# A decoder layer on one core: elementwise work leaves GpSimd, index look-up by a minimum, part of the one-hots on ScalarE

## Chip, core and metric

One core of a Trainium2 chip runs the whole layer as one program. The metric is the device time of one execution in microseconds (us), lower is better. The engines are named as in the profile: PE is TensorE's matmul stream and PEld its weight loads, DVE is VectorE, ACT is ScalarE, POOL is GpSimd, SP is SyncE, which here only issues DMAs.

## What is computed

The reference is one post-norm decoder layer over 512 tokens of width 2048, in float32. Cut to what matters here:

```python
x1 = layer_norm(ALPHA * x + mix)                       # mix: pooling and gated linear attention, projected
q = (x1 @ w_query).reshape(T, 8, 2, 128)               # 8 heads, two halves
s, idx = top_k(einsum(q, sub_keys), 16)                # 16 of 128 keys per half
top_s, sel = top_k(s[:, :, 0, :, None] + s[:, :, 1, None, :], 16)
expert = idx0[sel // 16] * 128 + idx1[sel % 16]        # 128 picks a token, of 16384 experts
gate = softmax(top_s)
h = gelu(einsum('tkd,td->tk', u_tab[expert], x1))
y = einsum('tk,tkd->td', gate * h, v_tab[expert])
ple = sigmoid(x1 @ ple_w_gate) * (p @ ple_w_proj)
out = layer_norm(ALPHA * x1 + y + ple)
```

## The kernel before

Every large float32 matrix product is made of three passes over rounded halves (`mm3`): ACT casts a loaded 128x1024 piece to its high part (`shi` or `bigh`, L74), DVE or POOL subtracts that from the piece to get the low part (`slo` or `bigl`, L75), and PE runs high-high, low-high and high-low. A piece that comes late in either half stops PE at L93 or L95.

The stages follow one another in the program, and a scheduler orders the instructions of each engine in advance; on the chip each engine runs its own list in order. What matters here:

- **Norm stage** (near 618 to 668 us). `layer_norm` runs on DVE (L363 multiplies by the weight, L364 adds the bias, 128x2048 each), and for the token block `tt == 1` the add runs on POOL. The low parts for the small products with `ple_proj` and for the query chunks are POOL's.
- **Query stage** (near 668 to 868 us). Sixteen feature chunks of 48 matmuls; their low parts are POOL's (`nc.gpsimd` in the call of `feature_chunk`). Beside it runs `select`, a generator that is advanced between half chunks: per head DVE finds the top 16 (L441 to L445), turns positions into numbers, and looks the key indices up with a one-hot: DVE compares (`oh`, L484), POOL multiplies by the indices (L486), DVE sums (L487). It ends in `eidx` (L490).
- **Gate stage** (near 868 to 1215 us). Sixteen chunks with `ple_gate` (`ple_block`), each followed by a sigmoid on ACT and by products and residual adds on DVE (L627 to L631). Between half chunks a hook advances `routing`: for each group of four tokens DVE makes gate one-hots A1 (four of L652) and index one-hots A2 (one L654), PE multiplies them (L668), ACT copies the result into `stage` (L669), and a DMA writes it to memory. Groups are made two ahead. The hook also takes 1.5 sparse steps: POOL gathers the 128 rows of one pick (L527, an indirect DMA), and DVE takes their dot product with x1 (L544).
- **Dense stage** (near 1235 to 3042 us). 128 experts' columns at a time, all products for tokens 192 to 511, with `LOOK = 4` pieces split ahead. Each piece is a tick that also takes about 0.68 sparse steps for tokens 0 to 191: 128 dots and 128 adds for the first set (128 tokens), 64 of each for the second set (64 tokens, two copies side by side on the partitions). `x` for the second set goes into the buffer (`xs`) of the first.
- **Tail**. `first_out` and `second_out` normalize the two sparse sets. The second one adds its two copies with a product with a `fold` matrix on PE. They stand near the end of the list of items; after the list three blocks of dense tokens are transposed, normalized (`finish`) and written.

Of the kernel before, what the change touches and what calls it, by code (L numbers as in the profile page):

```python
# [10 lines left out]
F32 = mybir.dt.float32  # L11
# [9 lines left out]
P = 128  # L21
T = 512
# [29 lines left out]
def layer_kernel(ctx: ExitStack, tc: tile.TileContext, I, out):  # L52
# [301 lines left out]
    def layer_norm(dst, src, stats, w, b, pool, add_eng=None):  # L354
# [9 lines left out]
        (add_eng or nc.vector).tensor_add(dst, dst, b)  # L364

    with tc.tile_pool(name="outp", bufs=2, reuse_waits="tile") as op, tc.tile_pool(name="outc", bufs=1, reuse_waits="tile") as oc:
# [4 lines left out]
        for nb in range(4):  # L371
            sl = slice(nb * 512, (nb + 1) * 512)
            pss = token_block(I["w_out"][nb], YTh, YTl, pre=mixed if nb == 0 else None)
            if nb == 0:
# [10 lines left out]
                split(pTh, pTl, load_half(I["pT"]).rearrange("p (c t) -> p c t", c=2), nc.gpsimd)  # L385
# [6 lines left out]
        for q in range(4):  # L392
            wh, wl = load_split(I["ple_proj"][q], nc.gpsimd)
# [40 lines left out]
    iota = load_const("iota", [P, P], pool=sc1)  # L434
    i1a = sc1.tile([P, NT, NPICK], F32, name="i1a")
# [12 lines left out]
    def select(hd, s):  # L448
# [7 lines left out]
        nc.vector.tensor_copy(sif, si)  # L456
# [75 lines left out]
    def sparse_steps():  # L532
# [20 lines left out]
        nc.sync.dma_start(out=x[0], in_=x1d[0])  # L553
        for j in range(NPICK):
            step("u_rows", eidx, j, dot(x, hcol, j))
            yield
        x = [None]
        for j in range(NPX):
            step("u_rows", eidx1, j, dot(x, hcol1, j, PX), PX)
            if j == NROW - 1:  # L560
                x[0] = sp_.tile([P, D], F32, tag="xs", name="xs")
                for k in range(REP):
                    nc.sync.dma_start(out=x[0][k * NX:(k + 1) * NX, :], in_=x1d[1, :NX, :])
                nc.scalar.activation(hcol, hcol, AF.Gelu)
            if j == 9:
                nc.vector.tensor_mul(hcol, hcol, gate0)
            yield
        for j in range(NPICK):
            step("v_rows", eidx, j, add(accs[0], hcol, j))
            if j == NROW:  # L570
# [3 lines left out]
                nc.scalar.activation(hcol1[:PX], hcol1[:PX], AF.Gelu)  # L574
            if j == 9:
                nc.vector.tensor_mul(hcol1[:PX], hcol1[:PX], gate1[:PX])
# [44 lines left out]

    def ple_block(nb):
        for j in range(4):
# [5 lines left out]
            for dst, cs in ((baseS[:, f, P:], slice(P, NS)), (baseT[:, f, :], slice(NS, T))):  # L629
                for xx in (x1h, x1l):  # L630
                    mark[0] = nc.vector.scalar_tensor_tensor(dst, xx[:, f, cs].bitcast(F32), ALPHA, dst,  # L631
                                                             op0=ALU.mult, op1=ALU.add)


    def routing(tt):
# [8 lines left out]
        i1T, i2T, gT = tps  # L644
        B4 = [P, 4, P]
        lane = iota.unsqueeze(1).broadcast_to(B4)

        def onehots(t0):
            A1 = rt.tile(B4, F32, name="A1", bufs=3)
            A2 = rt.tile(B4, F32, name="A2", bufs=3)  # L650
            for t in range(t0, t0 + 4):
                nc.vector.tensor_scalar(A1[:, t - t0, :], iota, i1T[:, t:t + 1], gT[:, t:t + 1],  # L652
                                        op0=ALU.is_equal, op1=ALU.mult)
# [63 lines left out]
    with ExitStack() as es:  # L717
# [9 lines left out]
        def paced_split(src):  # L727
# [8 lines left out]
            mark[0] = split(hi, lo, raw)  # L736
# [207 lines left out]
```

## Time and profile before

| | |
|---|---|
| time, median of 3 runs | 3084.13 us (3079.32 to 3084.88) |
| the profiled execution: time, span | 3077.86 us, 3076.1 us |
| PE busy | 2941.5 us of the span |
| DVE busy | 2395.9 us |
| ACT busy | 1057.9 us |
| POOL busy | 748.4 us |

The span is from the first to the last instruction, and 1.8 us of the execution lie outside it. Busy times are summed over stages that have different limits, so the shares say little by themselves: a stage is read from which engine is full in it and from what the others wait for.

### The profile page before, as it was taken

To read this page: it belongs to the slowest core of one execution; us is meant where nothing else is said; L and a number is where in the kernel's file an instruction comes from. 1 tells how busy PE (TensorE), PEld (TensorE's weight loads), DVE (VectorE), ACT (ScalarE), POOL (GpSimd) and SP (SyncE) were. 2 spreads that over 40 slices of the span, in tenths; PEclk is the share of its full clock that TensorE was granted. 3 is DMA by queue.
4 is the path that set the end of the run, shared out by engine and by line. 5 is a ranking of instruction groups with operands and counts; after the bars stand their busy time and mean duration, and the time that the engine had idled before them with its cause. 6 is when DMAs were issued, how large, how long until landed. Compare 5 with 4: busy or idle time off the path is not lost.

```text
span 3076.1 us, 44401 instructions
## 1 busy us (share of the span) xinstructions
PE 2941.5 (96%) x17637; PEld 2743.0 (89%) x17637; DVE 2395.9 (78%) x3468; ACT 1057.9 (34%) x1290; POOL 748.4 (24%) x474
## 2 busy tenths in 40 slices
PE   9999999989987888999999999999999999999996
PEld 7878788878766776999999999999999999999996
DVE  3353733268889998998897898898988888989876
ACT  3232331152222443433333333333333333433332
POOL 0000400045522112222223222222223223222210
PEclk9999999999998889999999999999999999999998
DMA  5222133332247677999999999999999999999982
GB/s 200 103 103 103 58 135 123 111 110 76 83 147 265 260 254 271 392 371 370 365 361 345 372 364 371 356 373 362 367 364 367 368 360 362 374 360 369 356 302 89
DMA packets 206657, 833.74 MB, mean 271 GB/s; under 512 B 19105, under 2 KB 60577, under 8 KB 153522
## 3 DMA queue, kind: packets, MB, share of 16 engines
q1 hardware_dynamic: 107058, 386.29, 34.3%
q0 software_dynamic: 55296, 402.68, 33.9%
q10 hardware_dynamic: 44096, 41.95, 4.1%
q8 instruction: 138, 2.26, 0.3%
q14 instruction: 69, 0.57, 0.1%
HBM read 800.36 MB, written 30.41 MB: 270 GB/s over the span
## 4 chain that ended last, share of the span: by engine, by line
PE 69%; issue 14%; DVE 9%; POOL 5%; DMA 2%; ACT 1%; POOLq 0%; ACTq 0%; SPq 0%; DVEq 0%
PE ps L95 22%; PE ps L93 22%; PE ps L94 22%; POOL row L527 4%; DMA row<-in_u_rows,eidx 2%; DVE row L544 2%; DVE A L652 2%; DVE A L654 1%; DVE slo L75 1%; PE ps L612 0%; DVE basev L363 0%; DVE attnT L242 0%; DVE basev L364 0%; DVE E L265 0%; ACT shi L74 0%
## 5 line engine op out<-in xcount | busy, mean ns | idle before, releaser
L74 ACT CAST shi<-raw 128x1024 fp32r<-128x1024 f32 x474 | 498.8, 1053 | 1210.5 <-PE ps L94 880.2
L75 DVE TENSOR_TENSOR slo<-raw,shi 128x1024 fp32r<-128x1024 f32 x438 | 533.9, 1222 | 418.8 <-ACT shi L74 411.3
L95 PE MATMUL ps<-bigh,slo 128*128 128x320 f32 (+1 forms) x2016 | 697.7, 346 | 40.1 <-DVE slo L75 33.5
L93 PE MATMUL ps<-bigh,shi 128*128 128x320 f32 (+1 forms) x2016 | 697.6, 346 | 11.1 <-ACT shi L74 7.3
L94 PE MATMUL ps<-bigl,shi 128*128 128x320 f32 (+1 forms) x2016 | 696.7, 346 | 0.0
L527 POOL DMA_INDIRECT row<-in_u_rows,eidx x192 | 274.5, 1430 | 791.9 <-DVE row L544 667.7
L544 DVE SCALAR_TENSOR_TENSOR row<-row,xs 128x2048 f32<-128x2048 f32 x192 | 438.0, 2286 | 29.7 <-DMA row<-in_u_rows,eidx 21.0
L527 POOL DMA_INDIRECT row<-in_v_rows,eidx x192 | 283.5, 1477 | 704.1 <-DVE acc L548 439.7
L95 PEld LDWEIGHTS ps<-bigh,slo 128*128 128x128 f32 x2016 | 384.7, 191 | 75.4 <-DVE slo L75 36.4
L93 PEld LDWEIGHTS ps<-bigh,shi 128*128 128x128 f32 x2016 | 384.7, 191 | 43.9 <-ACT shi L74 8.9
L94 PEld LDWEIGHTS ps<-bigl,shi 128*128 128x128 f32 x2016 | 384.5, 191 | 31.8 <-issue 0.9
L93 PE MATMUL ps<-ah,shi 128*128 128x320 f32 x1232 | 381.1, 309 | 0.0
L95 PE MATMUL ps<-ah,slo 128*128 128x320 f32 x1232 | 381.1, 309 | 0.0
L94 PE MATMUL ps<-al,shi 128*128 128x320 f32 x1232 | 381.1, 309 | 0.0
L74 ACT CAST bigh<-raw 128x1024 fp32r<-128x1024 f32 x216 | 226.7, 1051 | 402.6 <-PE ps L94 382.3
L75 DVE TENSOR_TENSOR bigl<-raw,bigh 128x1024 fp32r<-128x1024 f32 x216 | 263.4, 1222 | 80.6 <-ACT bigh L74 78.1
L548 DVE SCALAR_TENSOR_TENSOR acc<-row,hcol,acc 128x2048 f32<-128x2048 f32 x128 | 300.2, 2346 | 1.4 <-DMA row<-in_v_rows,eidx 1.1
L93 PE MATMUL ps<-bigh 128*128 128x320 f32 x816 | 252.1, 309 | 0.0
L94 PE MATMUL ps<-bigl,bigh 128*128 128x320 f32 x816 | 252.1, 309 | 0.0
L95 PE MATMUL ps<-bigh,bigl 128*128 128x320 f32 x816 | 252.1, 309 | 0.0
L93 PE MATMUL ps<-ah,bigh 128*128 128x320 f32 x816 | 252.1, 309 | 0.0
L94 PE MATMUL ps<-al,bigh 128*128 128x320 f32 x816 | 252.1, 309 | 0.0
(224 smaller groups left out, 4810.1 us busy)
## 6 DMA issues: line engine op xcount, KB each, us to landing
raw<-in_u_chunks SPq DMA_DIRECT2D x256, 512.0 KB
raw<-in_v_rows SPq DMA_DIRECT2D x256, 512.0 KB
gd<-stage ACTq DMA_DIRECT2D x20, 1024.0 KB
G<-gd ACTq DMA_DIRECT2D x16, 1280.0 KB
raw<-in_w_feat SPq DMA_DIRECT2D x34, 512.0 KB
raw<-in_w_tok SPq DMA_DIRECT2D x32, 512.0 KB
raw<-in_w_out SPq DMA_DIRECT2D x32, 512.0 KB
raw<-in_w_query SPq DMA_DIRECT2D x32, 512.0 KB
```

Of the source, the lines that this page charges most:

```text
L74: nc.scalar.copy(out=hi, in_=src)
L75: return (eng or nc.vector).tensor_sub(lo, src, hi.bitcast(F32))
L93: nc.tensor.matmul(ps, ah, bh, start=first, stop=False)
L94: nc.tensor.matmul(ps, ah, bl, start=False, stop=False)
L95: nc.tensor.matmul(ps, al, bh, start=False, stop=last)
L527: nc.gpsimd.indirect_dma_start(out=row[:n], out_offset=None, in_=I[table], in_offset=bass.IndirectOffsetOnAxis(ap=idx[:n, j:j + 1], axis=0))
L544: return lambda row: nc.vector.scalar_tensor_tensor(row, row, 1.0, x[0][:n], op0=ALU.mult, op1=ALU.mult, accum_out=h[:n, j:j + 1])
L548: return lambda row: nc.vector.scalar_tensor_tensor(acc[:n], row, h[:n, j:j + 1], acc[:n], op0=ALU.mult, op1=ALU.add)
L652: nc.vector.tensor_scalar(A1[:, t - t0, :], iota, i1T[:, t:t + 1], gT[:, t:t + 1], op0=ALU.is_equal, op1=ALU.mult)
L654: mark[0] = nc.vector.tensor_tensor(A2, lane, i2T[:, t0:t0 + 4].unsqueeze(2).broadcast_to(B4), op=ALU.is_equal)
```

## The change

No elementwise work runs on POOL from the output stage on: the low parts, the one bias add and the look-up product move to DVE. The look-up has no product any more: key indices get 512 times their position added, the wanted position is multiplied by 512, one subtraction is made, and a reduction takes the minimum of the absolute values. Every third group of gate one-hots is made on ACT, by `Abs(iota - index)` and `Relu(gate - 4 * that)`. The residual adds into `baseT` move from `ple_block` to the first 16 ticks of the dense stage. In the sparse steps six adds of the first set come ahead of the dots of the second, and GELU and gate product are cut so that they can. The second set is folded by a DMA and an add on DVE, and both outputs stand earlier in the list of items.

```diff
-        (add_eng or nc.vector).tensor_add(dst, dst, b)
+        nc.vector.tensor_add(dst, dst, b)
...
-            wh, wl = load_split(I["ple_proj"][q], nc.gpsimd)
+            wh, wl = load_split(I["ple_proj"][q])
...
+    steps512 = sc1.tile([P, TOPK], F32, name="steps512")
+    nc.vector.tensor_scalar(steps512, iota[:, :TOPK], 512.0, None, op0=ALU.mult)
...
-        nc.vector.tensor_copy(sif, si)
+        nc.vector.tensor_add(sif, si, steps512.unsqueeze(1).unsqueeze(1).broadcast_to([P, NT, 2, TOPK]))
...
+        nc.vector.tensor_scalar(abf[:, 0:2], abf[:, 0:2], 512.0, None, op0=ALU.mult)
...
-            nc.vector.tensor_tensor(oh, abf[:, pk].unsqueeze(3).broadcast_to(K2),
-                                    iota[:, :TOPK].unsqueeze(1).unsqueeze(1).broadcast_to(K2), op=ALU.is_equal)
-            nc.gpsimd.tensor_tensor(oh, oh, sif[:, :, pk, :].unsqueeze(2).broadcast_to(K2), op=ALU.mult)
-            nc.vector.tensor_reduce(dst[:, :, hs], oh, axis=AX.X, op=ALU.add)
+            nc.vector.tensor_sub(oh, sif[:, :, pk, :].unsqueeze(2).broadcast_to(K2),
+                                 abf[:, pk].unsqueeze(3).broadcast_to(K2))
+            nc.vector.tensor_reduce(dst[:, :, hs], oh, axis=AX.X, op=ALU.min, apply_absolute_value=True)
...
-        for j in range(NPX):
-            step("u_rows", eidx1, j, dot(x, hcol1, j, PX), PX)
-            if j == NROW - 1:
-                x[0] = sp_.tile([P, D], F32, tag="xs", name="xs")
...
+        for j in range(6):
+            step("v_rows", eidx, j, add(accs[0], hcol, j))
+            if j == NROW - 1:
+                x = [sp_.tile([P, D], F32, tag="xs", name="xs")]
+                for k in range(REP):
+                    nc.sync.dma_start(out=x[0][k * NX:(k + 1) * NX, :], in_=x1d[1, :NX, :])
+            yield
+        for j in range(NPX):
+            step("u_rows", eidx1, j, dot(x, hcol1, j, PX), PX)
...
-            ps = feature_chunk(I["w_query"][f], x1h, x1l, nc.gpsimd, lambda: advance(2))
+            ps = feature_chunk(I["w_query"][f], x1h, x1l, hook=lambda: advance(2))
...
-            for dst, cs in ((baseS[:, f, P:], slice(P, NS)), (baseT[:, f, :], slice(NS, T))):
-                for xx in (x1h, x1l):
-                    mark[0] = nc.vector.scalar_tensor_tensor(dst, xx[:, f, cs].bitcast(F32), ALPHA, dst,
-                                                             op0=ALU.mult, op1=ALU.add)
+            residual(baseS[:, f, P:], f, slice(P, NS))
...
+                if t0 // 4 % 3 == 0:
+                    nc.scalar.activation(A1[:, t - t0, :], iota, AF.Abs, bias=i1n[:, t:t + 1])
+                    nc.scalar.activation(A1[:, t - t0, :], A1[:, t - t0, :], AF.Relu, bias=gT[:, t:t + 1], scale=-4.0)
...
             mark[0] = split(hi, lo, raw)
+            if ticks[0] < ND:
+                residual(baseT[:, ticks[0], :], ticks[0], slice(NS, T))
...
-            src = [bank8() for _ in range(4)]
-            for b in range(4):
-                nc.tensor.matmul(src[b], tailc[0][:PX], accs[1][:PX, b * 512:(b + 1) * 512], start=True, stop=True)
-            finish([x[:NX] for x in src], NX, P)
+            acc = accs[1]
+            for k in range(1, REP):
+                part = acp.tile([P, D], F32, tag="row2", name="part", bufs=1)
+                nc.sync.dma_start(out=part[:NX], in_=acc[k * NX:(k + 1) * NX, :])
+                nc.vector.tensor_add(acc[:NX], acc[:NX], part[:NX])
+            finish([acc[:NX, b * 512:(b + 1) * 512] for b in range(4)], NX, P)
...
-        second = items.pop()
-        items.insert(len(items) - GRP // 2, second)
+        items.insert(len(items) - 2 * GRP + 2, (None, first_out))
+        items.insert(len(items) - 2 * GRP + 6, (None, second_out))
```

The order on DVE in the query stage, at the end of the selection for the first head (`oh` is the look-up table, `sco` the next head's scores), was before:

```order
L480 TENSOR_TENSOR abf<-abf 128x128
L484 TENSOR_TENSOR oh<-abf,c_iota 128x1024 x2
L487 TENSOR_REDUCE i1a<-oh 128x4x16
L487 TENSOR_REDUCE i2a<-oh 128x4x16
L441 MAX sv<-sco 128x8
L490 SCALAR_TENSOR_TENSOR eidx<-i2a,i1a 128x16
```

It is now:

```order
L481 TENSOR_TENSOR abf<-abf 128x128
L444 MATCH_REPLACE sco<-sv,sco 128x128
L482 TENSOR_SCALAR abf<-abf 128x128
L445 MAX sv<-sco 128x8
L486 TENSOR_TENSOR oh<-sif,abf 128x1024 x2
L488 TENSOR_REDUCE i1a<-oh 128x4x16
L488 TENSOR_REDUCE i2a<-oh 128x4x16
L446 MAX_INDEX si<-sv,sco 128x8
L491 SCALAR_TENSOR_TENSOR eidx<-i2a,i1a 128x16
L442 MAX sv<-sco 128x8
L75 TENSOR_TENSOR slo<-raw,shi 128x1024
```

The two look-up instructions and the two reductions stand as before, without POOL's product between them, and the low parts of the query chunks (`slo`) now stand between the selection's instructions.

ACT's list in the gate stage, at the first groups of routing, was before:

```order
L669 COPY stage<-ps 128x4x128 x4
L672 DMA gd<-stage 128x2048
L669 COPY stage<-ps 128x4x128
L74 CAST shi<-raw 128x1024
L669 COPY stage<-ps 128x4x128 x2
```

It is now, at the same place:

```order
L684 COPY stage<-ps 128x4x128
L664 ACTIVATE A_6656<-c_iota,i1n 128x128 x2
L665 ACTIVATE A_6656<-A_6656,gT 128x128 x2
L664 ACTIVATE A_6656<-c_iota,i1n 128x128 x2
L665 ACTIVATE A_6656<-A_6656,gT 128x128 x2
L684 COPY stage<-ps 128x4x128 x3
L687 DMA gd<-stage 128x2048
```

Eight short activations came in for each group that left DVE, 27 groups and 216 activations in all, between the copies that free PE's banks and the casts that feed it.

DVE's list in the dense stage, where the sparse steps go over to the second set (`hcol_4296`), was before:

```order
L785 TENSOR_TENSOR baseT<-baseT,ps 128x320 x6
L75 TENSOR_TENSOR bigl<-raw,bigh 128x8x128
L544 SCALAR_TENSOR_TENSOR row_12564,hcol_4296<-row_12564,xs 128x2048
L544 SCALAR_TENSOR_TENSOR row_12625,hcol_4296<-row_12625,xs 128x2048
L75 TENSOR_TENSOR slo<-raw,shi 128x1024
```

It is now:

```order
L549 SCALAR_TENSOR_TENSOR acc<-row_12871,hcol,acc 128x2048
L75 TENSOR_TENSOR bigl<-raw,bigh 128x8x128
L75 TENSOR_TENSOR slo<-raw,shi 128x1024
L549 SCALAR_TENSOR_TENSOR acc<-row_12905,hcol,acc 128x2048
L75 TENSOR_TENSOR slo<-raw,shi 128x1024
L545 SCALAR_TENSOR_TENSOR row_12983,hcol_4296<-row_12983,xs 128x2048
```

The first dot of the second set no longer follows the last dot of the first: six adds, which need no `xs`, stand between them. Counted over DVE's whole list, of the 32 residual adds into `baseT` 20 stood between the first and the last one-hot before and 6 do now; 9 now stand behind the first split of the dense stage that goes into `bigl`.

## Rows read from the trace of the kernel before

**Rows 1.** The page, part 1: busy us, share of the span, instructions.

```profile
PE 2941.5 (96%) x17637; PEld 2743.0 (89%) x17637; DVE 2395.9 (78%) x3468; ACT 1057.9 (34%) x1290; POOL 748.4 (24%) x474
```

**Rows 2.** Windows: stretch, length; busy PE, PEld, DVE, ACT, POOL (count); PEclk, DMA, GB/s.

```profile
668.00:868.00 200.00, 193.27 (x903) 157.91 (x903) 157.10 (x803) 50.74 (x64) 104.80 (x42) 1.00 0.24 84
868.00:903.00 35.00, 27.33 (x109) 21.92 (x107) 29.41 (x128) 10.24 (x11) 10.30 (x6) 0.85 0.25 91
...
930.00:1200.00 270.00, 219.83 (x1151) 188.01 (x1150) 258.83 (x571) 108.30 (x111) 59.78 (x38) 0.89 0.70 252
...
1672.00:3042.00 1370.00, 1366.33 (x9283) 1364.06 (x9283) 1192.34 (x1108) 485.79 (x585) 369.02 (x252) 1.00 0.93 353
3042.00:3076.00 34.00, 8.21 (x50) 6.62 (x47) 27.88 (x40) 11.67 (x19) 0.00 (x0) 0.64 0.31 108
```

**Rows 3.** Waits of PE, 668 to 1235 us: us in total, times, longest.

```profile
PE ps L95 <- DVE slo L75: 33.5, 10, 7.7
PE ps L668 <- DVE A L654: 21.8, 11, 4.4
...
PE ps L95 <- POOL slo L75: 6.6, 4, 1.8
```

**Rows 4.** Waits of DVE, 668 to 1235 us.

```profile
DVE i1a L487 <- POOL oh L486: 18.3, 8, 2.3
DVE row L544 <- DMA row<-in_u_rows,eidx: 17.1, 11, 3.4
...
DVE i2a L487 <- POOL oh L486: 9.1, 8, 1.2
```

**Rows 5.** Timeline of DVE, query stage: start us, us, instruction.

```profile
819.79 0.97 DVE L490 SCALAR_TENSOR_TENSOR eidx<-i2a,i1a 128x16 int32<-128x16 f32 x1
...
845.71 0.98 DVE L490 SCALAR_TENSOR_TENSOR eidx<-i2a,i1a 128x16 int32<-128x16 f32 x1
...
872.67 0.16 DVE L490 SCALAR_TENSOR_TENSOR eidx<-i2a,i1a 128x16 int32<-128x16 f32 x1
```

**Rows 6.** Timeline of DVE and POOL, norm stage.

```profile
630.40 2.29 DVE L364 TENSOR_TENSOR basev<-basev,c_ln_b 128x2048 f32<-128x2048 f32 x1
...
643.90 4.37 DVE L364 TENSOR_TENSOR basev<-basev,c_ln_b 128x2048 f32<-128x2048 f32 x1
...
641.66 13.15 POOL L75 TENSOR_TENSOR slo<-raw,shi 128x1024 fp32r<-128x1024 f32 x3
```

**Rows 7.** Timeline of DVE, gate stage.

```profile
1139.46 0.49 DVE L631 SCALAR_TENSOR_TENSOR baseT<-bigl,baseT 128x320 f32<-128x320 f32 x1
1139.87 1.23 DVE L75 TENSOR_TENSOR slo<-raw,shi 128x1024 fp32r<-128x1024 f32 x1
1141.00 1.12 DVE L652 TENSOR_SCALAR A<-c_iota,i1T,gT 128x128 f32<-128x128 f32 x4
1142.03 0.69 DVE L654 TENSOR_TENSOR A<-c_iota,i2T 128x512 f32<-128x512 f32 x1
```

**Rows 8.** Timeline of ACT, dense stage.

```profile
1646.51 0.31 ACT L564 ACTIVATE hcol<-hcol 128x128 f32<-128x128 f32 x1
```

**Rows 9.** Busy time in two stretches around the second set's first dot, and that dot on DVE.

```profile
1672.00:1696.00 24.00, 20.33 (x124) 20.10 (x124) 22.30 (x25) 7.16 (x8) 8.95 (x6) 0.87 1.01 414
1624.00:1648.00 24.00, 24.00 (x166) 24.00 (x165) 19.98 (x19) 8.47 (x10) 7.76 (x5) 1.00 1.03 381
...
1663.24 2.29 DVE L544 SCALAR_TENSOR_TENSOR row<-row,xs 128x2048 f32<-128x2048 f32 x1 [8.23 <-DMA xs<-x1d]
```

**Rows 10.** The tail: PE's fold in the chain, and DVE's timeline.

```profile
3035.63 1.72 PE ps L829 x4
...
3046.30 2.33 DVE L817 TENSOR_TENSOR raw<-raw,ln_w 64x1024 f32<-64x1024 f32 x2
3048.55 2.34 DVE L818 TENSOR_TENSOR raw<-raw,ln_b 64x1024 f32<-64x1024 f32 x2
3050.82 0.15 DVE L808 RECIPROCAL rstd<-rstd 128x1 f32<-128x1 f32 x1
```

More of the change, by code (lines that the diff above doesn't have):

```diff
@@ L352, in layer_kernel, with layer_norm @@
     x1d = dram.tile([2, P, D], F32, name="x1d")
-    def layer_norm(dst, src, stats, w, b, pool, add_eng=None):
+    def layer_norm(dst, src, stats, w, b, pool):
         mv = pool.tile([P, 2], F32, name="mv")
@@ L384, in layer_kernel @@
                 pTl = pc.tile([P, 2, T], F32R, name="pTl")
-                split(pTh, pTl, load_half(I["pT"]).rearrange("p (c t) -> p c t", c=2), nc.gpsimd)
+                split(pTh, pTl, load_half(I["pT"]).rearrange("p (c t) -> p c t", c=2))
             for tt in range(NT):
@@ L402, in layer_kernel @@
         for tt in range(NT):
-            layer_norm(base[:, tt, :], base[:, tt, :], stats[:, tt], lnw, lnb, op,
-                       nc.gpsimd if tt == 1 else nc.vector)
+            layer_norm(base[:, tt, :], base[:, tt, :], stats[:, tt], lnw, lnb, op)
             if tt < 2:
@@ L553, in sparse_steps, with gelu @@
         nc.sync.dma_start(out=x[0], in_=x1d[0])
+        def gelu(h, g, c0, c1, n=P):
+            nc.scalar.activation(h[:n, c0:c1], h[:n, c0:c1], AF.Gelu)
+            nc.vector.tensor_mul(h[:n, c0:c1], h[:n, c0:c1], g[:n, c0:c1])
+        cut = NPICK - TOPK
         for j in range(NPICK):
             step("u_rows", eidx, j, dot(x, hcol, j))
+            if j == cut + NROW:
+                gelu(hcol, gate0, 0, cut)
             yield
-        x = [None]
+        for j in range(6):
[5 more added lines that the diff above has]
+            yield
         for j in range(NPX):
             step("u_rows", eidx1, j, dot(x, hcol1, j, PX), PX)
-            if j == NROW - 1:
-                x[0] = sp_.tile([P, D], F32, tag="xs", name="xs")
[L562 to L566, printed above, removed]
+            if j == NROW:
+                gelu(hcol, gate0, cut, NPICK)
             yield
-        for j in range(NPICK):
+        for j in range(6, NPICK):
             step("v_rows", eidx, j, add(accs[0], hcol, j))
-            if j == NROW:
+            if j == 6 + NROW:
                 accs.append(sp_.tile([P, D], F32, tag="xs", name="xs"))
@@ L573, in sparse_steps @@
                 nc.sync.dma_start(out=accs[1][:NX, :], in_=y1d)
[L574 to L576 removed]
+                gelu(hcol1, gate1, 0, NPX, PX)
             yield
@@ L619, in layer_kernel, with residual @@
     free.extend(((sp_, "row0"), (sp_, "row1")))
+    def residual(dst, f, cs):
+        for xx in (x1h, x1l):
+            mark[0] = nc.vector.scalar_tensor_tensor(dst, xx[:, f, cs].bitcast(F32), ALPHA, dst,
+                                                     op0=ALU.mult, op1=ALU.add)
     def ple_block(nb):
@@ L644, in routing @@
         i1T, i2T, gT = tps
+        i1n = rt.tile([P, P], F32, name="i1n", bufs=1)
+        nc.vector.tensor_scalar(i1n, i1T, -1.0, None, op0=ALU.mult)
         B4 = [P, 4, P]
@@ L791, in tail_consts @@
             if not tailc:
-                tailc.append(load_const("fold", [P, P], pool=sp_))
                 for nm, tag in (("ln2_w", "row0"), ("ln2_b", "row1")):
@@ L796, in tail_consts @@
                     tailc.append(t)
-            return tailc[1:]
+            return tailc
         def finish(src, rows, t0):
@@ L913, in _arrays @@
     j = np.arange(P)
-    A["fold"] = (j[:, None] % NX == j[None, :]).astype(np.float32)
     A["iota"] = c(np.broadcast_to(np.arange(P, dtype=np.float32), (P, P)))
```

7 lines of the change are left out of this document (3 added, 4 removed).

## The prediction, made before the changed kernel ran

> **What bounds the kernel now.** I read four views, from the coarse to the fine.
>
> The page's first part comes first [rows 1]: PE is busy for 96% of the span and DVE for 78%. That is an average, so the second view is the busy time by stretch [rows 2]. In the dense stretch, 1672 to 3042 us, PE has 1366.3 of 1370 us at full clock. It is the bound there, and DVE's 1192 us are hidden: what the change does to DVE or POOL in this stretch is worth nothing. Four other places can give something. In the query stretch (668 to 868) PE has 193.3 of 200 us, DVE 157. In the next 35 us PE has only 27.3. In the gate stretch (930 to 1200) DVE is full, 258.8 of 270 us (96%), while PE's 219.8 us stand at a granted clock of 0.89, which is 195.6 us of work at full clock. In the tail (3042 to 3076) PE has 8.2 us, DVE 27.9.
>
> The third view says for whom PE waits between 668 and 1235 us [rows 3]: 33.5 us for DVE's low parts (`slo`), 21.8 us for its index one-hots, 6.6 us for POOL's low parts. The fourth, DVE's own waits in the same stretch [rows 4]: 18.3 + 9.1 us for POOL's look-up product and 17.1 us for gathered rows. So from 668 to 1215 us the end is set by DVE, and by POOL where DVE waits for it.
>
> **The change part by part.**
>
> *Norm stage.* The bias add of 128x2048 takes DVE 2.29 us by itself and 4.37 us while POOL makes three low parts in 13.15 us [rows 6]; four of DVE's passes over 2048 elements are of the slow kind (4.3 to 4.5 us). With POOL idle they should take the short time: 4 x 2.1 = -8.4 us. DVE takes over the add of `tt == 1` (2.3) and five low parts. A low part costs DVE 1.13 us from start to start (1139.87 to 1141.00 [rows 7]): 5.7 us. Sum -8.4 + 2.3 + 5.7 = -0.4, taken as 0. Bounds: -5 if the low parts fall into DVE's gaps, +4 if only half of the slowing goes.
>
> *Selection.* One head takes DVE 25.92 us (`eidx` at 819.79 to `eidx` at 845.71 [rows 5]). Its waits for POOL go: (18.3 + 9.1)/8 = 3.4 us [rows 4]. Its last instruction should fall from 0.97 us to 0.16, which is what the third one took, when no POOL work was in flight [rows 5]: 0.8 us. The multiplication by 512 and the add in place of a copy add some 0.3 us. So DVE gives back 8 x 3.9 = 31 us. It takes over 27 low parts within the selection: 27 x 1.13 = 30.5 us. Between heads with four of them the period becomes 25.92 - 3.9 + 4.5 = 26.5 us; over the whole, about -1 us. The two sides cancel since the selection on DVE already sets the end of the query stage: PE runs ahead of it and then stands in the 35 us behind 868 [rows 2, 3]. POOL's 104.8 busy us of this stretch [rows 2] go, but they were no bound. Bounds: -5 (the look-up's other instructions were slowed too), +12 (rival 2).
>
> *Gate stage.* One group's four gate one-hots cost DVE 1.03 us (1141.00 to 1142.03 [rows 7]), and 27 of the 80 groups leave it: -27.8 us. Of the residual adds 14 leave this stage, each 0.41 us (1139.46 to 1139.87 [rows 7]): -5.7. The negated indices add three small instructions, 0.6 us. DVE's load falls by 32.9, to 226 us, which is still above PE's 195.6, so DVE stays the bound. It will not get all of it: it idles 11.2 of 270 us now, the rows gathered by POOL come no sooner (17.1 us of waits for them in 547 us of query and gate stages [rows 4]), and as the two engines come closer each hand-over costs more. I give back 7 and take -26 us. Bounds: -33 (nothing given back), -10 (rival 3 in part).
>
> What ACT pays: 216 activations of 128x128. No such one-hot is in the trace; the row of the same shape and engine is 0.31 us [rows 8], so 67 us. ACT's 108.3 us in this stretch [rows 2] become 175 in some 240: not full. A whole group's eight take 2.5 us, and groups are made two ahead, so I cost them at nothing on the path. The cover is this lead; without it rival 1 holds.
>
> Against this part speaks a rule of the Trainium skill, "ScalarE: Activation LUTs", section "Rules for kernel authors": relu and the like belong on VectorE, and an ACTIVATE is to be budgeted at about 0.3 us and some 0.83 ns for an element of the row. That would be an estimate of 0.41 us each, 88 us in all, and ACT at 196 us: by the page, too, it is not full, but its bursts would be 3.3 us long. The row says 0.31, and the row's price stands in the sum.
>
> *Start of the dense stage.* Nine residual adds now lie behind the first dense split: 9 x 0.4 = 3.6 us on DVE, which has 22.3 of 24 us just there [rows 9]. Four pieces split ahead cover most of it. +1 us (0 to +4).
>
> *Second set.* Its first dot waits 8.23 us for `xs`, and DVE's list, low parts included, stands behind it [rows 9]. In the 24 us from 1672, just behind, PE does 124 matmuls at a granted clock of 0.87, in an undisturbed stretch 166 [rows 9]: 42 missing x 24/166 us = 6.1 us. Now six adds that don't need `xs` stand between (six of about 2.3 us, as the dot beside them, with low parts between), so the transfer has its time. -6 us (-6 to 0: the wait for the dots of the first set before the buffer is free could come back in a shorter form).
>
> *Tail.* PE's fold leaves the chain: groups of four of its matmuls stand there with 1.72 us [rows 10], two of them, -3.4 us. The second set's multiply and add stand between the first dense block's work and its reciprocal: 3046.30 to 3050.82 [rows 10], 4.5 us, and with both outputs earlier that is done while PE is still busy. -8 us (-4 if the outputs' DMAs, now ahead of the last loads in SP's queue, hold a piece up; four pieces of lookahead at some 3.5 us each stand against that).
>
> **Sum.** 0 - 1 - 26 + 1 - 6 - 8 = -40 us. The profiled execution took 3077.9 us (its span and 1.8 us outside it), so 3037.9. The median of the runs shown is 3084.1, 6.2 above the profiled one, and I forecast against that: **3044 us**.
>
> **Rivals.**
>
> *Rival 1, slower: ACT's bursts are on PE's path.* ACT's list is in order, and in the new order eight activations stand between the copies that free PE's banks and the casts that feed it. If each of the 27 groups holds PE up by its full 8 x 0.31 = 2.5 us, and DVE is not slow enough to hide it, that is +67 us against -40: 3111 us. It decides from 40/27 = 1.5 us a group upward. For it speaks that a cast is waited for as a low part is. Against it: ACT has 162 idle us of 270 in this stretch [rows 2], PE's listed waits there are for DVE [rows 3], and what the page's rule calls wrong is a price per element, not a place in the queue. By the page's 3.3 us a group (88 us in all) it would be 3132 us. Chance 0.06.
>
> *Rival 2: the query stage stretches.* POOL made low parts beside DVE's work; now each one waits its turn behind some selection instructions, and PE, which has 193.3 of 200 us there [rows 2], waits for it. If the stretch of 200 us takes the 8 x 26.5 = 212 of the selection and the 35 us behind it don't shrink in return, that is +12, and +4 for the norm stage: 3060 us. For it: waits for POOL's low parts are only 6.6 us now, those for DVE's 33.5 [rows 3]. Against it: the same selection must end in either case before PE goes on. Chance 0.15.
>
> *Rival 3: gathered rows become the bound of the gate stage.* Dots take rows in two buffers, and DVE already waits for them [rows 4]; the DMA engines are busy 0.70 of the stretch [rows 2]. If DVE's gain is turned into such waits, 27 of the 33 us go, 20 more than the 7 in the sum: 3044 + 20 = 3064 us. Against it: POOL, which issues the gathers, has only 59.8 busy us [rows 2] and now nothing else to do. Chance 0.13.
>
> That nothing is gained (new waits in the gate stage eat all of it and the rest cancels) has 0.04.
>
> **How the numbers follow.** The forecast has 0.62; 3044 is its time. With the gate stage at -33 and the norm and query stages at -5 each the sum is -56, 3028; the single runs shown lie up to 5 us from their median: low end 3024. The high end takes in rivals 2 and 3 with a few us more, 3070. Beyond it lie rival 1, the case of no gain, and rivals 2 and 3 together. A measurement of this kernel can tell about 0.2% (6 us) from no change. Forecast, rivals 2 and 3 are all faster, 0.90 less 0.02 for several at once: 0.88; same 0.05; slower 0.07.
>
> **What would show it.** Norm: all bias adds at 2.3 us. Selection: `eidx` to `eidx` near 26.5 us, no wait for POOL. Gate: the stage shorter by some 26 us, DVE still over 90% busy, ACT near 175 us; waits for `shi` or `A` on ACT would be rival 1, longer ones of the dots for `row` rival 3. Second set: no wait of 8 us for `xs`, and near 166 matmuls in 24 us. Tail: no fold on PE, 5 to 8 us less behind the last dense product. The prediction is wrong if DVE isn't what limits the gate stage, or if removing POOL's work does not speed up DVE's passes.

## The result and the profile after

The changed kernel takes 3041.64 us (median of 4 runs, 3040.3 to 3043.58) against 3083.81 us before (4 runs): the ratio is 0.9866, 95% interval 0.9849 to 0.9884, a gain of 42 us. Forecast were 3044 us, with a range of 3024 to 3070. The profiled execution took 3042.6 us with a span of 3040.6, so the two profiled spans are 35.5 us apart; single runs of either kernel differ by several us.

Page, part 1, and busy time by stretch, columns as in [rows 1, 2]. They answer to those rows; the last two stretches are 24 us around the second set's first dot [rows 9] and the tail.

```profile
PE 2921.8 (96%) x17629; PEld 2730.3 (90%) x17629; DVE 2393.1 (79%) x3412; ACT 1114.3 (37%) x1507; POOL 602.4 (20%) x420
...
668.00:868.00 200.00, 195.69 (x909) 160.09 (x907) 185.75 (x864) 51.80 (x65) 2.29 (x2) 0.99 0.26 91
868.00:903.00 35.00, 32.99 (x137) 26.83 (x138) 34.93 (x123) 11.28 (x12) 1.68 (x1) 0.95 0.38 131
...
930.00:1200.00 270.00, 217.97 (x1201) 186.50 (x1201) 241.30 (x471) 163.39 (x323) 66.03 (x43) 0.90 0.77 285
...
1660.00:1684.00 24.00, 24.00 (x165) 24.00 (x165) 24.00 (x31) 7.82 (x11) 8.39 (x6) 1.00 0.99 391
...
3005.00:3041.00 36.00, 12.00 (x84) 10.95 (x82) 25.88 (x40) 9.01 (x15) 0.00 (x0) 0.67 0.22 88
```

DVE is now nearly full in the query stretch (185.75 us, before 157.1), PE hardly stands behind it any more (33.0 of 35 us, before 27.3), and the 24 us at the second set's start are whole: 165 matmuls at full clock.

The shares don't say where the 35.5 us are. For that the timeline gives instants that both kernels have: the sigmoids of the gate stage (ACT, 16 of them) and the activations of the dense stage (ACT, `act<-ps`, 128 of them). From their start times in each profile:

| stretch | before | after | difference | forecast |
|---|---|---|---|---|
| start to first sigmoid (norm, query) | 888.7 | 879.0 | -9.7 | -1 |
| first to last sigmoid (gate) | 325.6 | 296.4 | -29.1 | -26 |
| last sigmoid to 7th dense activation | 66.0 | 82.7 | +16.7 | +1 |
| 7th to 30th | 330.9 | 330.9 | 0 | 0 |
| 30th to 42nd (second set begins) | 203.4 | 197.1 | -6.3 | -6 |
| 42nd to 128th | 1168.6 | 1168.6 | 0 | 0 |
| 128th to the end (tail) | 93.0 | 85.9 | -7.1 | -8 |

The two stretches of the dense stage in which neither kernel changes sets are the same to 0.1 us. One term of the forecast is far out: the start of the dense stage.

Waits of PE and of DVE, 600 to 1240 us (us in total, times, longest), the kernel after; they answer to [rows 3, 4].

```profile
PE ps L95 <- DVE slo L75: 22.1, 9, 4.9
PE ps L683 <- DVE A L669: 21.6, 9, 8.8
PE ps L93 <- ACT shi L74: 16.8, 2, 11.5
...
PE ps L683 <- ACT A L665: 1.5, 4, 0.7
```

```profile
DVE slo L75 <- ACT shi L74: 42.2, 11, 5.5
DVE row L545 <- DMA row<-in_u_rows,eidx: 21.2, 16, 3.1
```

No wait for POOL is left on either engine. New is PE's 16.8 us for `shi` (two waits). For ACT's one-hots PE waits 1.5 us: rival 1 did not come.

Timeline of DVE, norm stage and two heads' ends in the query stage (start, us, instruction); they answer to [rows 5, 6].

```profile
638.65 2.29 DVE L364 TENSOR_TENSOR basev<-basev,c_ln_b 128x2048 f32<-128x2048 f32 x1
...
644.26 2.29 DVE L364 TENSOR_TENSOR basev<-basev,c_ln_b 128x2048 f32<-128x2048 f32 x1
...
658.28 2.29 DVE L364 TENSOR_TENSOR basev<-basev,c_ln_b 128x2048 f32<-128x2048 f32 x1
...
814.26 0.16 DVE L491 SCALAR_TENSOR_TENSOR eidx<-i2a,i1a 128x16 int32<-128x16 f32 x1
...
840.14 0.16 DVE L491 SCALAR_TENSOR_TENSOR eidx<-i2a,i1a 128x16 int32<-128x16 f32 x1
```

All passes over 2048 elements take 2.29 us now, and `eidx` takes 0.16 us. The period of a head is 25.88 us (840.14 - 814.26).

### The profile page after: what moved, and what is told of

It is laid out like the page before. It is cut to its first block, busy times and chain, and to the rows that moved or that the text cites. A ratio compares the mean times of both kernels' runs of the same rounds, so it can differ in the third digit from the quotient of the medians.

```text
span 3040.6 us, 44461 instructions
## 1 busy us (share of the span) xinstructions
PE 2921.8 (96%) x17629; PEld 2730.3 (90%) x17629; DVE 2393.1 (79%) x3412; ACT 1114.3 (37%) x1507; POOL 602.4 (20%) x420
## 4 chain that ended last, share of the span: by engine, by line
PE 80%; DVE 12%; issue 3%; DMA 3%; ACT 1%; POOL 1%; SPq 0%; ACTq 0%; DVEq 0%; POOLq 0%
PE ps L93 26%; PE ps L95 26%; PE ps L94 26%; DMA row<-in_u_rows,eidx 2%; DVE row L545 2%; DVE slo L75 2%; DVE A L667 1%; DVE oh L486 1%; DVE A L669 1%; DVE si L443 1%; DVE sco L444 1%; DVE si L446 0%; DMA raw<-in_u_chunks 0%; DVE sv L445 0%; POOL row L528 0%
## 5 line engine op out<-in xcount | busy, mean ns | idle before, releaser
L75 DVE TENSOR_TENSOR slo<-raw,shi 128x1024 fp32r<-128x1024 f32 x474 | 578.5, 1222 | 443.0 <-ACT shi L74 435.3
L93 PE MATMUL ps<-bigh,shi 128*128 128x320 f32 (+1 forms) x2016 | 696.2, 345 | 16.8 <-ACT shi L74 16.8
```

The costliest lines, as they stand in the source:

```text
L75: return (eng or nc.vector).tensor_sub(lo, src, hi.bitcast(F32))
L93: nc.tensor.matmul(ps, ah, bh, start=first, stop=False)
```

## The start of the dense stage, where the forecast missed

ACT's and SP's timeline between the last sigmoid (L638) and the first dense activation (L777), the kernel after:

```profile
1175.43 0.58 ACT L638 ACTIVATE ps<-ps 128x512 f32<-128x512 f32 x1 [10.30 <-PE ps L95]
...
1187.57 0.58 ACT L721 COPY raw<-ps 64x512 f32<-64x512 f32 x1 [8.52 <-PE ps L718]
1187.63 0.38 ACTq L760 DMA_DIRECT2D G<-gd  x1
1191.72 1.04 ACT L74 CAST shi<-raw 128x1024 fp32r<-128x1024 f32 x1 [3.57 <-DMA raw<-in_u_chunks]
1200.05 1.04 ACT L74 CAST shi<-raw 128x1024 fp32r<-128x1024 f32 x1 [7.28 <-DMA raw<-in_u_chunks]
...
1217.42 0.44 ACT L777 ACTIVATE act<-ps 128x320 f32<-128x320 f32 x1
```

```profile
1179.63 1.08 SPq L82 DMA_DIRECT2D raw<-in_u_chunks  x1
1188.18 0.45 SPq L722 DMA_DIRECT2D y1d<-raw  x1
1188.71 37.37 SPq L82 DMA_DIRECT2D raw<-in_u_chunks  x13
```

Only one load of the dense stage is issued ahead of the fourth write of `y1d`, which stands behind ACT's copy at 1187.57. The loads then land slowly: ACT's cast of the second piece waits 7.28 us. How full the DMA engines are shows in the windows (columns as in [rows 2]):

```profile
1190.00:1200.00 10.00, 0.90 (x2) 0.50 (x2) 5.62 (x6) 1.04 (x1) 3.68 (x2) 0.50 1.02 370
1200.00:1210.00 10.00, 4.78 (x18) 4.78 (x19) 3.67 (x3) 4.16 (x4) 0.00 (x0) 0.50 1.01 387
```

They are full (1.02 and 1.01) while PE does 20 matmuls in 20 us, with a granted clock of 0.50 (its lower level, 1.2 GHz), after it had stood nearly still. Part of that traffic are the rows of the sparse dots, one megabyte each: 7 dots start between the last sigmoid and the first dense activation, before it were 3. The queue of POOL's gathers (packets, MB, share of the 16 DMA engines) moved this between the two instants, first in the kernel before (1214 to 1243 us), then in the kernel after (1175 to 1218 us):

```profile
q0 software_dynamic: 488, 3.58, 35.2%
```

```profile
q0 software_dynamic: 983, 7.13, 44.5%
```

At the 370 to 387 GB/s of the windows the 3.55 MB more are some 9 us of transfers, an estimate.

## Experiments

The table has for each run its stretches (us, from the instants above; "dots" are the dots that start between the last sigmoid and the first dense activation), the span, and the median with its ratio to the kernel before on the same chip. The kernel before had a median of 3083.8 us on the chip of `after`, 3078.9 on that of e1 to e4, 3081.5 for e5 to e8, 3081.2 for e9 to e11 and 3082.2 for e12. Medians from two chips therefore compare only to about 5 us; the ratios allow for that.

| run | to first sigmoid | gate | to first dense act. (dots) | 1st to 128th act. | tail | span | median | ratio (95%) |
|---|---|---|---|---|---|---|---|---|
| before | 888.7 | 325.6 | 28.0 (3) | 1740.9 | 93.0 | 3076.1 | 3083.8 | |
| after | 879.0 | 296.4 | 42.0 (7) | 1737.3 | 85.9 | 3040.6 | 3041.6 | 0.9866 (0.9849 to 0.9884) |
| e1 | 879.6 | 311.2 | 27.6 (3) | 1737.1 | 84.9 | 3040.3 | 3045.5 | 0.9895 (0.9879 to 0.9912) |
| e2 | 878.7 | 312.9 | 35.8 (6) | 1748.3 | 85.3 | 3061.0 | 3050.7 | 0.9908 (0.9891 to 0.9924) |
| e3 | 869.6 | 293.8 | 39.3 (6) | 1739.0 | 84.9 | 3026.7 | 3028.9 | 0.9839 (0.9823 to 0.9856) |
| e4 | 879.0 | 296.7 | 42.7 (7) | 1737.2 | 86.3 | 3041.8 | 3044.2 | 0.9884 (0.9864 to 0.9903) |
| e5 | 879.5 | 299.2 | 32.7 (3) | 1737.6 | 85.3 | 3034.3 | 3034.1 | 0.9849 (0.9830 to 0.9868) |
| e6 | 880.0 | 258.6 | 34.7 (6) | 1734.2 | 85.0 | 2992.4 | 2995.0 | 0.9727 (0.9709 to 0.9744) |
| e7 | 880.1 | 299.1 | 37.1 (7) | 1741.6 | 84.9 | 3042.9 | 3048.1 | 0.9895 (0.9878 to 0.9911) |
| e8 | 880.7 | 296.5 | 39.4 (7) | 1737.3 | 93.9 | 3047.8 | 3051.2 | 0.9909 (0.9892 to 0.9926) |
| e9 | 868.8 | 257.5 | 34.4 (6) | 1733.5 | 85.0 | 2979.1 | 2983.8 | 0.9685 (0.9669 to 0.9701) |
| e10 | 868.2 | 250.2 | 32.8 (5) | 1772.1 | 85.4 | 3008.7 | 3010.6 | 0.9766 (0.9746 to 0.9785) |
| e11 | 868.5 | 277.4 | 39.8 (6) | 1735.0 | 85.0 | 3005.7 | 3006.7 | 0.9755 (0.9732 to 0.9778) |
| e12 | 867.6 | 259.6 | 33.8 (5) | 1739.9 | 83.8 | 2984.7 | 2990.3 | 0.9703 (0.9687 to 0.9719) |

### e1: residual adds back in the gate stage

```diff
             residual(baseS[:, f, P:], f, slice(P, NS))
+            residual(baseT[:, f, :], f, slice(NS, T))
...
-            if ticks[0] < ND:
-                residual(baseT[:, ticks[0], :], ticks[0], slice(NS, T))
```

> The changed kernel with the residual adds into baseT put back into the blocks with ple_gate. In the changed kernel the last sigmoid comes 38.8 us earlier than before, but the first dense activation only 24.8 and the seventh 22.1 us earlier: 16.7 us are lost between. Theory A (the moved adds and the dots stand on DVE ahead of what the first dense pieces need): from the last sigmoid to the seventh dense activation falls from 82.7 us to about 70, the gate stage gets 4 to 6 us longer, time 3032 to 3038 us. Rival B (the first dense loads come late for another reason): the stretch stays at 81 to 84 us, the gate stage gets 4 to 6 us longer, time 3044 to 3049 us.

The stretch from the last sigmoid to the seventh dense activation fell to 68.0 us, as theory A had it; but the gate stage got 14.7 us longer, not 4 to 6, and the span is the same to 0.3 us. The time fell in B's range, and between the medians (3045.5 and 3041.6) the intervals of the ratios overlap. By the trace DVE was busy for 8.6 us more of the gate stage and idle for 6.2 us more. So moving the adds is worth little or nothing here: with them the stage ends later, with 45 dots in it and 3 behind it; without them it ends earlier, with 44 in it and 7 behind. What the gate stage seems to gain by the move, the start of the dense stage loses.

### e2: all gate one-hots on VectorE

```diff
-                if t0 // 4 % 3 == 0:
+                if False:
```

> The changed kernel with all gate one-hots on VectorE. Theory (DVE sets the gate stage, ACT's 67 us cost nothing on the path): the gate stage, first to last sigmoid, goes from 296.4 us to 318 to 324, and 20 to 27 us of it reach the end: 3062 to 3069 us. Rival (ACT's bursts hold PE up by as much as DVE saves, and the residual adds and the quieter POOL made the gain): the gate stage stays within 6 us, 3036 to 3048 us.

The gate stage is 16.5 us longer (expected 22 to 28) and the median 9.1 us, 13 us by the ratios. The third on ACT is worth that: the theory in kind, less in size, for 3050.7 us lies below the 3062 to 3069 that it expected. Why the stage gains less than DVE sheds shows in the gate window of e2 and in DVE's waits for gathered rows, e2 and then the kernel after; the same window of the kernel after stands under e6.

```profile
880.00:1191.00 311.00, 260.74 (x1353) 222.13 (x1352) 298.21 (x658) 118.94 (x124) 67.93 (x45) 0.91 0.71 260
```

```profile
DVE row L545 <- DMA row<-in_u_rows,eidx: 8.9, 5, 3.3
```

```profile
DVE row L545 <- DMA row<-in_u_rows,eidx: 18.1, 13, 3.1
```

DVE's busy time falls by 30.2 us, from 298.21 to 267.96, but its idle time rises from 12.8 to 27.0 us, and 9.2 of these 14.2 us are waits for rows. That is rival 3 in part. The span of its profile, 20.4 us longer, isn't used for the price: that execution took 3062.9 us and the other three 3049.6 to 3050.9, and 11.0 us of the excess lie in the dense stage (1748.3 for 1737.3 us). The sizes in the gate stage add up: 16.5 us for the one-hots and 14.7 for the adds (e1) against 29.1 in all. And ACT paid what was worked out: in the kernel after, a window (900 to 1200 us, the one-hots of ACT alone; busy us and count) has

```profile
900.00:1200.00 300.00, 66.81 (x216) 0.90 0.78 288
```

### e3: low parts of the query stage back on GpSimd

```diff
-            wh, wl = load_split(I["ple_proj"][q])
+            wh, wl = load_split(I["ple_proj"][q], nc.gpsimd)
...
-            ps = feature_chunk(I["w_query"][f], x1h, x1l, hook=lambda: advance(2))
+            ps = feature_chunk(I["w_query"][f], x1h, x1l, nc.gpsimd, lambda: advance(2))
```

(and the same for `pT`.)

> The changed kernel with the low parts of the query chunks, of ple_proj and of pT on GpSimd again; the look-up by a minimum stays. Theory (the low parts cost DVE about what a quiet GpSimd gives back, so that this edit is worth nothing by itself): last eidx within 4 us of the changed kernel's 893.5, time 3038 to 3046 us. Rival (GpSimd's elementwise work was what held the query stage, by slowing DVE's passes): four norm passes at 4.3 us again, last eidx 5 to 10 us later, 3047 to 3052 us. Second rival (the low parts now burden DVE, which is full there): last eidx 10 us or more earlier, 3025 to 3035 us.

The second rival: last `eidx` at 883.1 us, 10.4 us earlier, and 12.7 us off the median (8 us by the ratios), although two of the norm stage's adds are slow again (4.34 and 4.37 us). The same stretch in three kernels, before, after and e3 (columns as in [rows 2]):

```profile
700.00:860.00 160.00, 153.27 (x716) 124.92 (x715) 138.06 (x713) 41.22 (x52) 90.58 (x36) 1.00 0.24 82
```

```profile
700.00:860.00 160.00, 156.29 (x726) 127.89 (x725) 159.11 (x748) 40.66 (x52) 1.21 (x1) 0.99 0.25 87
```

```profile
700.00:860.00 160.00, 159.86 (x754) 131.63 (x753) 158.18 (x770) 43.39 (x55) 62.90 (x26) 1.00 0.26 92
```

Before, DVE had 22 us of idle time, most of it waits for POOL's product [rows 4]. After, it is full with low parts, and PE waits a little. In e3 the low parts cost POOL 2.4 us each beside it (62.90 for 26), a head takes 23.84 us, and PE is full. The look-up by a minimum alone is thus worth about 2 us a head, and the low parts on DVE take that back.

### e4: writes of y1d on ACT's queue

```diff
-                nc.sync.dma_start(out=y1d[:, bs], in_=sg[:n, :512])
+                nc.scalar.dma_start(out=y1d[:, bs], in_=sg[:n, :512])
```

> The changed kernel with the four writes of y1d issued by ScalarE instead of SyncE. Theory (the first dense loads stand in SP's queue behind the fourth write, which waits for DVE): loads are issued some 8 us earlier, the first dense activation comes 34 to 36 us behind the last sigmoid instead of 42, time 3032 to 3036 us. Rival (the DMA engines are full there, and loads land no sooner): 40 us or more, 3039 to 3044 us.

No gain (42.7 us, 3044.2), as the rival had it. The run tells less than was meant, since ACT got a stall of its own (its timeline, e4):

```profile
1185.45 0.38 ACTq L760 DMA_DIRECT2D G<-gd  x1
1186.00 17.60 ACTq L722 DMA_DIRECT2D y1d<-raw  x1
1203.64 2.94 ACT L74 CAST shi<-raw 128x1024 fp32r<-128x1024 f32 x3 [17.67 <-issue]
1206.48 1.04 ACT L74 CAST bigh<-raw 128x1024 fp32r<-128x1024 f32 x1
1211.05 1.05 ACT L74 CAST bigh<-raw 128x1024 fp32r<-128x1024 f32 x1 [3.52 <-DMA raw<-in_u_chunks]
```

The issue of the fourth write, behind the large load of `G`, held ACT for 17.6 us. Still the fifth piece is cast at 1211.05, with a wait for its load, while in the kernel after it was cast at 1208.98, though SP had issued the twelve loads from 1181.9 on, 6.8 us earlier than the thirteen there. That speaks for full DMA engines as the limit; whether SP's order alone matters stays open.

### e5: no dots in the last four hooks of the gate stage

```diff
-        early(1 + hooks[0] % 2)
+        if hooks[0] <= 28:
+            early(1 + hooks[0] % 2)
```

> The changed kernel without the sparse steps of the last four hooks of the gate stage (six dots, which the dense stage takes over). From the last sigmoid to the first dense activation it was 28.0 us with 3 dots before, 27.6 with 3 dots when the residual adds were put back, and 42.0 with 7 dots in the changed kernel. Theory (the megabyte of rows that each of these dots gathers competes with the first dense loads): with 3 dots or fewer there, 25 to 31 us, and the first dense activation 8 to 14 us earlier; time 3028 to 3034 us. Rival (the stretch is long because the gate stage ends early against something with its own pace, a sum of about 324 us from the last eidx to the first dense activation): that sum stays above 320 us, time 3038 to 3044 us.

Three dots are left there, and the stretch falls from 42.0 to 32.7 us, above the expected 31. The first dense activation comes only 6.0 us earlier, where 8 to 14 were expected, the seventh 12.1 us, and the sum from the last `eidx` is 317.2 us. The runs e4, e7 and e8, which start as many dots there as the kernel after, differ by several us in this stretch (37.1 to 42.7), but their seventh activation comes at 1257.1 to 1258.9 us, in e5 at 1246.0. So the dots do hold up the dense start, by 11 to 13 us at the seventh activation. The edit takes their rows from the DMA engines and their time from DVE at once. ACT's fourth copy, behind which the fourth write of `y1d` stands, comes 4.8 us after the last sigmoid here and 12.1 in the kernel after:

```profile
1183.52 0.58 ACT L722 COPY raw<-ps 64x512 f32<-64x512 f32 x1 [0.30 <-PE ps L719]
```

So which share is the rows' stays open. Of the gain 6.2 us went again between the 30th and the 42nd activation (203.3 us): DVE waited 6.9 us for rows of the adds and 4.2 us for `G` there. The median is 3034.1; by the ratios, whose intervals overlap with those of the kernel after, the gain is not clear of noise. Over all runs of the table the stretch goes with the dots, though a longer stretch also leaves room for more dots to start: 27.6 to 32.7 us with 3, 32.8 and 33.8 with 5, 34.4 to 39.8 with 6, 37.1 to 42.7 with 7.

### e6: one dot for a hook

```diff
-        early(1 + hooks[0] % 2)
+        early(1)
```

> The changed kernel with one sparse step for a hook of the gate stage in place of 1.5: 32 steps of the 384 there, and the dense stage takes over 16. Theory (DVE sets the gate stage, 2.3 us a dot, and the dense stage has room for them): first to last sigmoid from 296.4 us to 265 to 278, and less competition with the first dense loads; time 3010 to 3025 us. Rival (the dense stage, whose DMA engines are at 0.94, pays for 16 more rows): the gain is met by 10 us or more behind the first dense activation, 3028 to 3040 us.

Beyond the theory: 13 fewer dots start in the gate stage (31 for 44), it falls by 37.8 us to 258.6 (2.9 us a dot), and the dense stage, which got 16 more, is not longer. The gate stage, kernel after and e6:

```profile
880.00:1175.00 295.00, 254.25 (x1355) 216.67 (x1354) 267.96 (x542) 175.01 (x340) 66.65 (x45) 0.93 0.73 272
```

```profile
880.00:1138.00 258.00, 242.88 (x1359) 208.91 (x1358) 244.46 (x536) 175.14 (x341) 33.04 (x31) 0.98 0.70 257
```

PE needs 243 us for the same matmuls and gets 258; at a granted clock of 0.98 they also take 11 us less than at 0.93. DVE's busy time falls by 23.5 us and its idle time by 13.5, of which 11.8 are waits for rows (18.1 us in the kernel after, shown under e2):

```profile
DVE row L545 <- DMA row<-in_u_rows,eidx: 6.3, 4, 2.9
```

So the limit of the gate stage after the change was DVE together with the rows that its dots wait for, and here DVE and PE are level.

### e7 and e8: old order of the sparse steps; old fold and tail

e7 puts the generator of sparse steps back as before (no six adds ahead of the second set); e8 puts back the product with `fold` and the places of the two outputs.

```diff
-        for j in range(6):
-            step("v_rows", eidx, j, add(accs[0], hcol, j))
...
+        x = [None]
         for j in range(NPX):
             step("u_rows", eidx1, j, dot(x, hcol1, j, PX), PX)
```

```diff
-            acc = accs[1]
...
-            finish([acc[:NX, b * 512:(b + 1) * 512] for b in range(4)], NX, P)
+            src = [bank8() for _ in range(4)]
+            for b in range(4):
+                nc.tensor.matmul(src[b], tailc[0][:PX], accs[1][:PX, b * 512:(b + 1) * 512], start=True, stop=True)
+            finish([x[:NX] for x in src], NX, P)
...
-        items.insert(len(items) - 2 * GRP + 2, (None, first_out))
-        items.insert(len(items) - 2 * GRP + 6, (None, second_out))
+        second = items.pop()
+        items.insert(len(items) - GRP // 2, second)
```

> The changed kernel with the sparse steps in the order of before (no six adds ahead of the second set's dots). Theory (the wait for xs, with low parts queued behind it, cost PE some 6 us): between the 30th and the 42nd dense activation 203.4 us as before, in the changed kernel 197.1; time 3045 to 3050 us. Rival (that stretch got shorter since the whole stage came at another moment): 197 to 198 us, and 3039 to 3043 us.

> The changed kernel with the fold on TensorE and the places of the two outputs as before. Theory (the tail's 7.1 us are the fold on PE, 3.4 us, and the second set's elementwise work in the last chain): from the last dense activation to the end of the span 92.9 us as before, in the changed kernel 85.9; time 3047 to 3052 us. Rival (only one of the two was on the path): 88 to 90 us, and 3043 to 3047 us.

e7: the wait is back on DVE, and between the 30th and the 42nd activation it is 201.4 us, between the two expectations (203.4 and 197.1); the median is 3048.1, as the theory had it, though the interval of its ratio overlaps with that of the kernel after.

```profile
1639.26 2.29 DVE L545 SCALAR_TENSOR_TENSOR row<-row,xs 128x2048 f32<-128x2048 f32 x1 [7.39 <-DMA xs<-x1d]
```

e8: the tail is 93.9 us, all of the gain is gone, and the median is 3051.2. The second set's weight and bias passes stand again between the last product and the first dense block's reciprocal, at 3017.05 and 3019.31 us:

```profile
3014.00 0.14 DVE L825 RECIPROCAL rstd<-rstd 64x1 f32<-64x1 f32 x1
...
3017.05 2.33 DVE L834 TENSOR_TENSOR raw<-raw,ln_w 64x1024 f32<-64x1024 f32 x2
3019.31 2.35 DVE L835 TENSOR_TENSOR raw<-raw,ln_b 64x1024 f32<-64x1024 f32 x2
3021.58 0.15 DVE L825 RECIPROCAL rstd<-rstd 128x1 f32<-128x1 f32 x1
```

### e9 to e12: how far it goes

e9 has e3's and e6's edits together. The other three change one thing in it:

```diff
e10:
-        early(1)
+        early(hooks[0] % 2)
e11:
-                if t0 // 4 % 3 == 0:
+                if t0 // 4 % 2 == 0:
e12:
-        early(1)
+        if hooks[0] <= 28:
+            early(1)
```

> The changed kernel with both edits that paid so far: the low parts of query chunks, ple_proj and pT on GpSimd, and one sparse step for a hook. By itself the first brought the median 12.7 us down and the second 46.7. Theory (they act in different stages, on DVE's load in the query stage and in the gate stage): they add up, 2980 to 2986 us, last eidx at 883 to 885 us. Rival (with fewer dots PE is the limit of the gate stage, 242.9 busy of 258 us, and what comes early from the query stage is lost at the first dense loads): 2987 to 2995 us.

> As the run before, with a sparse step only at every second hook, 16 of the 384 in the gate stage. Theory (PE is the limit of the gate stage at one step for a hook already): first to last sigmoid falls by at most 10 us more, and the dense stage, which takes 16 more rows at a DMA share of 0.94, is longer by up to 10: within 8 us of the run before. Rival (DVE still limits the gate stage): 15 to 30 us faster.

> The kernel with both edits and every second group of gate one-hots on ScalarE in place of every third. Theory (with one step for a hook DVE no longer limits the gate stage, so ACT's share is of no more use, while 13 more bursts of 2.5 us stand ahead of copies and casts): the same within 4 us, or slower by up to 10. Rival (DVE still limits): 5 to 12 us faster.

> The kernel with low parts on GpSimd and one sparse step for a hook, now without the steps of the last four hooks: 28 of the 384 in the gate stage. With 32 there PE stood 5.8 us for its first dense piece and the last sigmoid lay 34.4 us ahead of the first dense activation, with 6 dots between; with 16 there the dense stage got 38.6 us longer (1772.1 against 1733.5 us from the first to the last dense activation). Theory (dots behind the last sigmoid hold up the first dense loads, and the dense stage has room for four more): 3 dots and 27 to 33 us there, the dense stage within 3 us, 2974 to 2981 us. Rival (the dense stage is at its limit at 32 already): 4 to 12 us longer there, 2985 to 2995 us.

e9 is the best kernel of the study: 2983.8 us, ratio 0.9685 (0.9669 to 0.9701), and the edits add up nearly (11.2 us off e6's median, 12.7 alone; by the ratios 13 and 8).

e10 is 27 us slower. The gate stage gains 7.2 us, as expected of a PE that is the limit; but the dense stage is 38.6 us longer, where at most 10 were expected. Its waits of PE there (1215 to 2920 us):

```profile
PE ps L93 <- DVE baseT L802: 21.5, 10, 5.4
PE ps L95 <- DVE bigl L75: 3.9, 2, 2.5
```

The dense stage takes 16 more steps for nothing and not 32: DVE comes late with the sums that free PE's banks. The two waits are 25.4 of the 38.6 us; the rest is not put down to anything here.

e11 is 23 us slower, all in the gate stage (277.4 against 257.5 us): neither expectation, both of which were within 12 us. Here rival 1's mechanism is to be seen. Windows of e9 and of e11:

```profile
930.00:1120.00 190.00, 181.28 (x1068) 157.60 (x1067) 182.71 (x390) 147.38 (x294) 22.47 (x22) 0.99 0.73 267
```

```profile
930.00:1120.00 190.00, 171.21 (x987) 146.02 (x985) 156.80 (x328) 166.46 (x378) 19.00 (x18) 0.97 0.67 243
```

and waits of PE, e11, 870 to 1195 us:

```profile
PE ps L718 <- DVE baseS L639: 9.9, 1, 9.9
PE ps L95 <- DVE slo L75: 9.6, 7, 4.1
PE ps L683 <- ACT A L665: 7.7, 4, 6.1
```

ACT is busy for 166 of 190 us, DVE for only 157, and PE waits 7.7 us for one-hots of ACT (0.5 in e9). DVE is held up in turn: it waits 21.9 us until PE has read an earlier one-hot (1.5 in e9):

```profile
DVE A L667 <- PE ps L683: 21.9, 10, 4.5
```

The rest of the 20 us isn't one wait, and its split is not settled.

e12 is the rival: one dot fewer behind the last sigmoid and 0.6 us, but 6.4 us more in the dense stage, and a median of 2990.3. Fewer than 32 steps in the gate stage are thus no better (e10, e12); between 32 and 48 no run was made.

## Why the prediction was right, point by point

**What bounds the kernel** was read rightly. Only the four places named moved, and the dense stage's inner stretches are equal to 0.1 us. That DVE sets the gate stage is shown by e2 and e6, together with the rows that its dots wait for, which the forecast counted within the 7 us that it gave back.

**Norm stage and selection** (0 and -1 forecast): -9.7 us to the first sigmoid. The first `eidx` came 4.3 us earlier, near the lower bound of the norm stage (-5); from the first to the last `eidx` it took 4.8 us less, which is at the selection's bound of -5. The heads' period was forecast as 26.5 us and is 25.88: DVE's idle time fell from some 3.5 us a head to 0.1 (22 and 0.9 us of 160), as forecast, and where the other 0.6 us come from is not shown. e3 shows what stood behind the small sum: two large terms of opposite sign, and the one with the wrong sign (the low parts, 10.4 us by the last `eidx`) could be left out. The slow passes of the norm stage fit a rule of the Trainium skill, "SBUF — State Buffer", section "SBUF: two separate sides": a DVE operation with two operands in the on-chip memory and a GpSimd operation that reads it take turns, each for a whole instruction. The trace agrees: 2.29 us alone, 4.34 to 4.37 beside POOL's low parts in e3.

**Gate stage** (-26): -29.1 us, within its bounds. Between the first and the last sigmoid DVE was busy for 301.3 us before and for 269.4 after, 31.9 less where 32.9 were forecast. Its two terms were mis-sized against each other: the one-hots gave 16.5 us of the 27.8 taken off DVE, the rest mostly turning into waits (e2), the adds 14.7 us for 5.7 (e1). One dot more in the stage with the adds back, 2.9 us by e6, explains a part of that; the rest is not settled.

**ACT's price** was right to 0.2 us: 66.8 us for 216. The budget of the Trainium skill, "ScalarE: Activation LUTs", section "Rules for kernel authors", would give an estimate of 88; the measured price decides. That section's advice to keep relu and the like on VectorE did not hold where VectorE sets the end and ScalarE idles (e2); at half of the groups, with ACT at 88% and DVE at 83% of a window, it did (e11).

**Start of the dense stage** (+1, bounds 0 to +4): the failed step. It looked at the nine adds on DVE and at the cover of four pieces. It did not ask what a gate stage that ends sooner leaves behind it: four more dots, whose rows go through the DMA engines just when the first dense pieces are to be loaded (7.13 MB of them for 3.58 before). The stretch came out 16.7 us longer. e5 shows the dots' part, 11 to 13 us by the seventh activation, with their rows and their time on DVE together; e4 speaks for the rows, and the remaining share is open.

**Second set** (-6): -6.3, and **tail** (-8): -7.1. Both confirmed by putting the old code back (e7 4.3 us in the stretch, e8 8.0). The prediction read the fold as two groups of four matmuls; the chain has one of four and two of two, 3.6 us in all for the 3.4 in the sum. e8 puts fold and places back together, so their shares are not separated.

**The sum** of -40 met -35.5 between the profiled spans and -42.2 between the medians. That it came so near is luck in part: misses of +15.7 and of -8.7 and -3.1 us met. Of the rivals, 3 came nearest. In the gate stage DVE's waits for rows took part of what the one-hots gave (e2, e6), though the stage still got 29.1 us shorter; and the same gathers stood in the hand-over behind it, where the rival did not look.

## What to carry to other kernels

Work that is taken off one engine is worth what the stage's limit allows, and what the next stage's first loads lose must be counted with it: ask what transfers cross the border between two stages once the first ends sooner. When all of an engine's elementwise work is moved, cost each part of the move by itself; here the look-up's move gained and the low parts' move lost, in the same stretch. The largest lever was in neither: how many sparse steps the gate stage takes and how many the dense stage (e6), up to the point at which the dense stage takes no more for nothing (e10; e12 by 6.4 us).

## What the hardware showed that was not expected

The issue of a small DMA from ACT behind a 1280 KB load on the same queue held ACT for 17.6 us (e4). A 128x1024 low part takes POOL 2.4 us beside DVE's selection (e3, and the same in the kernel before), not the 4.4 us that it takes beside DVE's passes over 2048 elements [rows 6], so what POOL's work costs there depends on what DVE does at the same time.
